# Tying DRAM-to-DRAM copies and accumulating DMAs of the up-projection's weights to their places in the ScalarE and GpSimd streams

## The chip, the core and the metric

The kernel runs on one core of a Trainium2 chip. The core has five engines that run their own instruction streams in order: TensorE (PE in the profile, its weight loads PEld), VectorE (DVE), ScalarE (ACT), GpSimd (POOL) and SyncE (SP). ACT, POOL and SP can issue DMAs, which run on the core's 16 DMA engines. The metric is the device time of one execution in microseconds; the number quoted is the median of several runs.

## The reference

A two-layer encoder on 1024 tokens of width 1024. Each layer adds three sub-layers to x: a mixer (latent attention, grouped-query attention and a gated MLP behind one input projection), cross-attention to 256 memory rows, and a gated feed-forward network (FFN) with a convolution over three tokens. The change touches the weights of the FFN's first product:

```python
def conv_gated_ffn(h, w_up, conv_w, conv_b, w_down):
    a = h @ w_up
    ap = jnp.pad(a, ((0, 0), (1, 1), (0, 0)))
    a = ap[:, :-2] * conv_w[0] + ap[:, 1:-1] * conv_w[1] + ap[:, 2:] * conv_w[2] + conv_b
    gate, val = a[..., :D_FF], a[..., D_FF:]
    return (jax.nn.silu(gate) * val) @ w_down

for l in range(DEPTH):
    x = x + hybrid_mixer(rms_norm(x, mix_norm[l]), ...)
    x = x + memory_cross_attention(rms_norm(x, mem_x_norm[l]), mem, ...)
    x = x + conv_gated_ffn(rms_norm(x, ffn_norm[l]), ffn_w_up[l], ...)
```

## The kernel before

All matrix products are done on pairs of rounded operands: a float32 tile is split into a high part (ACT or POOL copies it to the type fp32r) and a low part (DVE subtracts), and three matmuls add up one product (mm3, lines 113 to 115). `load` (lines 99 to 110) brings a weight tile in: SP issues the DMA (L103), POOL (L107) or ACT (L105) makes the high part, DVE (L108) the low part.

A layer runs in this order. First the opening: the input projection in four column groups, for the gated MLP (w_m; `gm_cols`, L414 to L424), keys and values (w_kv, L471), queries (w_q, L509) and the latent ranks (w_a, L543 to L548), with norms and rotary turns in between. Every norm needs a reciprocal root, which POOL computes as a power (L129, L560) from a DVE result and DVE then multiplies in (L420, L257, L563). Then the attention: 24 items of 512 queries and one head, 12 grouped-query and 12 latent ones; each item scores four tiles on PE (L733 and L734 for the first 12), takes the exponential on ACT (L296), scales by the sum on POOL (L302), transposes on PE (L137) and multiplies by the values (L315, L316). An item ends with L323 and L324 on ACT and L325 on POOL. Work for later items is filled in between from a table (`fill`). Then come the output projection, the memory attention and the FFN.

The FFN's up-projection is done with seven block products instead of eight (L1104 to L1106). The weights of products 1, 2 and 4 are blocks of w_up as they stand; those of 5, 6, 7 and 3 are sums of blocks: 5 is block 2 plus block 3, 6 is block 0 plus sum 5, 7 is block 0 plus block 2, and 3 is block 1 plus sum 6. These sums are made in DRAM, without any engine's arithmetic: `up_copy` (L778) has ACT issue a copy of one block's piece into a DRAM tile u, and `up_add` (L781) has POOL issue a DMA that adds another piece to it. Each sum is cut into six pieces, so a layer has 24 copies and 24 adds, of 512 KB or 1 MB. The FFN later reads u through SP (L1050).

In the code, the copies and adds are called inside the attention: `extra` gives step n (of 24) its copy in item n*5//6 and its add four items later, after the third tile of that item. The order of the instruction streams is not the order of the code, though: the framework's scheduler puts each engine's instructions in an order of its own, by priority and by when it reckons that their operands are there. A copy reads an input and writes a DRAM tile that nothing else uses before it, so for the scheduler it can go at any time. DMAs from ACT and SP share eight semaphore lanes; an issue that takes a lane waits for the DMA that had that lane before.

Of the kernel before, what the change touches and what calls it, by code (L numbers as in the profile page):

```python
# [11 lines left out]
ALU = mybir.AluOpType  # L12
# [57 lines left out]
def trunk(ctx: ExitStack, tc: tile.TileContext, a: dict, out: bass.AP):  # L70
    nc = tc.nc
# [319 lines left out]
    def layer(l, nt, last):  # L391
# [380 lines left out]
        up_sum = {(m, i): dpool.tile([P, n * CH + 16], F32, tag=f"u{l}_{m}_{i}", name=f"u{l}_{m}_{i}")[:, : n * CH] for m in (5, 6, 7, 3) for i, n in enumerate(UP_PARTS)}  # L772

        def up_piece(b, i):
            return a["w_up"][l, b][:, up_at[i] * CH : (up_at[i] + UP_PARTS[i]) * CH]

        def up_copy(m, i):
            nc.scalar.dma_start(up_sum[m, i], up_piece({5: 2, 6: 0, 7: 0, 3: 1}[m], i))  # L778

        def up_add(m, i):  # L780
            nc.gpsimd.dma_start(up_sum[m, i], {5: lambda: up_piece(3, i), 6: lambda: up_sum[5, i], 7: lambda: up_piece(2, i), 3: lambda: up_sum[6, i]}[m](), accum_op=ALU.add)  # L781

        def up_block(m, j):
            if m in (1, 2, 4):
# [58 lines left out]
        for n, (m, i) in enumerate(up_steps):  # L843
            extra.setdefault(n * 5 // 6, []).append(lambda m=m, i=i: up_copy(m, i))
            extra.setdefault(n * 5 // 6 + 4, []).append(lambda m=m, i=i: up_add(m, i))
# [537 lines left out]
```

## Time and profile before

| | us |
|---|---|
| median of 3 runs | 3009.76 |
| lowest, highest run | 3007.4, 3012.34 |
| the profiled execution, its span | 3010.89, 3008.9 |
| PE busy (share of the span) | 2807.4 (93%) |
| DVE, ACT, POOL busy | 1955.9, 1339.3, 650.0 |
| bytes moved by DMA | 297.61 MB, mean 99 GB/s |

The profile divides the span into 40 slices of 75 us and gives each engine's busy share, the clock that TensorE was granted (PEclk) and the use of the DMA engines. It lists instructions by line of the kernel; "s<-u" is a DMA from a DRAM tile u to a slot s. For each idle stretch of an engine it names the instruction or DMA that ended it. The times of layer 0 and of layer 1 can be set side by side, since both layers have the same code.

### The profile page before, as it was taken

The numbers are of one execution on the slowest core, as the hardware profiler recorded it, in microseconds if no ns is written. First come the engines' busy times: TensorE is split into PE (matmuls) and PEld (weight loads), VectorE is DVE, ScalarE is ACT, GpSimd is POOL, SyncE is SP. The second block draws the span as 40 slices with busy tenths as digits, with TensorE's granted clock in tenths as the row PEclk, the third lists the DMA queues.
The fourth block names the chain that finished last, engine by engine and source line by source line (L and its number), as shares of the span: only waits on it lengthen the run. The fifth ranks groups of instructions, "written<-read, shape, count | busy, mean of one in ns | idle before, by whom it ended". The sixth has DMA issues, their size and how long they took to land. (4 is left out here: it accounts for less than half of the span.)

```text
span 3008.9 us, 37081 instructions
## 1 busy us (share of the span) xinstructions
PE 2807.4 (93%) x13909; PEld 2358.4 (78%) x13909; DVE 1955.9 (65%) x2825; ACT 1339.3 (45%) x2572; POOL 650.0 (22%) x628
## 2 busy tenths in 40 slices
PE   3766499999999999999999999999999999999999
PEld 2656378888887888888888988888888788888887
DVE  2223489895667777777435489888466977778634
ACT  1212389882346444442104378985234644443101
POOL 2223245652200000002102245555111000001100
PEclk6878799999999999999999999999999999999999
DMA  9999920001211433334211000001111333335311
GB/s 311 256 251 265 245 72 1 1 29 57 71 57 56 143 121 123 126 130 171 98 42 39 23 14 1 1 8 50 53 54 59 110 126 125 120 121 191 123 56 56
DMA packets 93635, 297.61 MB, mean 99 GB/s; under 512 B 10384, under 2 KB 11024, under 8 KB 83216
## 3 DMA queue, kind: packets, MB, share of 16 engines
q1 hardware_dynamic: 79488, 202.70, 20.0%
q0 software_dynamic: 6912, 46.14, 7.8%
q10 hardware_dynamic: 7056, 46.40, 4.1%
q8 instruction: 110, 1.80, 0.2%
q14 instruction: 69, 0.57, 0.1%
HBM read 267.94 MB, written 119.54 MB: 129 GB/s over the span
## 5 line engine op out<-in xcount | busy, mean ns | idle before, releaser
L113 PE MATMUL bank<-s,s 128*128 128x512 f32 (+4 forms) x1831 | 684.8, 375 | 64.7 <-DVE s L121 36.3
L114 PE MATMUL bank<-s,s 128*128 128x512 f32 (+4 forms) x1831 | 678.8, 371 | 8.7 <-DVE s L108 8.7
L115 PE MATMUL bank<-s,s 128*128 128x512 f32 (+4 forms) x1831 | 679.7, 371 | 1.5 <-DVE s L108 1.4
L107 POOL TENSOR_SCALAR s<-s 128x1024 fp32r<-128x1024 f32 (+1 forms) x114 | 134.9, 1187 | 1456.0 <-DMA s<-in_w_down 1016.9
L113 PEld LDWEIGHTS bank<-s,s 128*128 128x128 f32 x1831 | 350.4, 192 | 121.8 <-DVE s L121 37.5
L114 PEld LDWEIGHTS bank<-s,s 128*128 128x128 f32 x1831 | 350.2, 191 | 60.2 <-DVE s L108 9.1
L137 PE MATMUL bank<-ident,s 128*128 128x128 f32 (+1 forms) x2320 | 321.9, 277 | 79.9 <-DVE stat L128 19.7
L121 DVE TENSOR_TENSOR s<-bank,s 128x512 fp32r<-128x512 f32 (+3 forms) x552 | 330.9, 630 | 99.7 <-ACT s L120 96.5
L115 PEld LDWEIGHTS bank<-s,s 128*128 128x128 f32 x1831 | 349.9, 191 | 54.6 <-DVE s L108 1.8
L120 ACT ACTIVATE s<-bank 128x512 fp32r<-128x512 f32 (+3 forms) x552 | 285.4, 555 | 207.1 <-PE bank L137 142.4
L137 PEld LDWEIGHTS bank<-ident,s 128*128 128x128 f32 (+1 forms) x2320 | 272.2, 141 | 134.2 <-issue 41.0
L108 DVE TENSOR_TENSOR s<-s,s 128x1024 fp32r<-128x1024 f32 (+4 forms) x172 | 214.3, 1255 | 125.4 <-POOL s L107 110.6
L1105 PE MATMUL bank<-s,s 128*128 128x512 f32 x704 | 274.5, 390 | 0.9 <-DVE s L206 0.9
L1106 PE MATMUL bank<-s,s 128*128 128x512 f32 x704 | 273.9, 389 | 0.0
L1104 PE MATMUL bank<-s,s 128*128 128x512 f32 x704 | 273.7, 389 | 0.0
L366 DVE TENSOR_TENSOR x<-x,bank 128x512 f32<-128x512 f32 x214 | 145.6, 684 | 193.4 <-PE bank L115 192.8
L302 POOL TENSOR_SCALAR s<-s,stat 128x1024 f32<-128x1024 f32 x192 | 218.5, 1141 | 224.3 <-DVE stat L301 156.3
L292 DVE TENSOR_REDUCE stat<-pair 128x1 f32<-128x1024 f32 x192 | 234.0, 1219 | 43.3 <-PE pair L734 23.3
L1057 ACT ACTIVATE s<-s 128x512 fp32r<-128x512 f32 x308 | 188.2, 628 | 162.7 <-PE bank L1106 49.7
L105 ACT ACTIVATE s<-s 128x1024 fp32r<-128x1024 f32 (+3 forms) x58 | 58.2, 1005 | 366.8 <-DMA s<-g 149.3
L296 ACT ACTIVATE s<-pair,stat 128x1024 f32<-128x1024 f32 x192 | 214.9, 1119 | 11.1 <-DVE stat L301 5.1
L1058 DVE TENSOR_TENSOR s<-s,s 128x512 fp32r<-128x512 f32 x308 | 201.8, 689 | 24.8 <-ACT s L1057 21.6
(164 smaller groups left out, 4659.8 us busy)
## 6 DMA issues: line engine op xcount, KB each, us to landing
s<-u SPq DMA_DIRECT2D x176, 256.0 KB, 3.0
u<-in_w_up ACTq DMA_DIRECT2D x40, 1024.0 KB, 19.2
s<-in_w_up SPq DMA_DIRECT2D x132, 256.0 KB, 3.2
g<-s SPq DMA_DIRECT2D x44, 512.0 KB, 2.8
s<-in_w_down SPq DMA_DIRECT2D x44, 512.0 KB, 4.8
s<-g SPq DMA_DIRECT2D x44, 512.0 KB, 5.6
u<-in_w_up POOLq DMA_DIRECT2D x20, 1024.0 KB, 18.4
u<-u POOLq DMA_DIRECT2D x20, 1024.0 KB, 19.8
```

The costliest lines, as they stand in the source:

```text
L113: nc.tensor.matmul(o, l[0], r[0], start=first, stop=False)
L114: nc.tensor.matmul(o, l[0], r[1], start=False, stop=False)
L115: nc.tensor.matmul(o, l[1], r[0], start=False, stop=last)
L120: nc.scalar.activation(hi, src, AF.Copy)
L121: nc.vector.tensor_tensor(lo, src, f(hi), ALU.subtract)
L137: nc.tensor.transpose(b[:m, j * P : (j + 1) * P], s, ident)
L292: nc.vector.reduce_max(self.nm[:, 0:1], s, axis=AX.X, negate=True)
L296: nc.scalar.activation(p, self.s, AF.Exp, bias=self.nm[:, 0:1], accum_out=self.den[:, t : t + 1])
L302: nc.gpsimd.tensor_scalar(p, p, r[:, 0:1], 0.0, ALU.mult, ALU.add)
L1104: nc.tensor.matmul(o, lh, rh, start=k == 0 and m in (1, 5, 6), stop=False, skip_group_check=True)
L1105: nc.tensor.matmul(o, lh, rl, start=False, stop=False, skip_group_check=True)
L1106: nc.tensor.matmul(o, ll, rh, start=False, stop=k == 3, skip_group_check=True)
```

## The change

Both DMA calls are handed to `tc.keep_in_program_order`, which holds an instruction at its place in its engine's stream: what the code issues on that engine ahead of it stays ahead, and what it issues behind it stays behind.

```diff
         def up_copy(m, i):
-            nc.scalar.dma_start(up_sum[m, i], up_piece({5: 2, 6: 0, 7: 0, 3: 1}[m], i))
+            tc.keep_in_program_order(nc.scalar.dma_start(up_sum[m, i], up_piece({5: 2, 6: 0, 7: 0, 3: 1}[m], i)))
 
         def up_add(m, i):
-            nc.gpsimd.dma_start(up_sum[m, i], {5: lambda: up_piece(3, i), 6: lambda: up_sum[5, i], 7: lambda: up_piece(2, i), 3: lambda: up_sum[6, i]}[m](), accum_op=ALU.add)
+            tc.keep_in_program_order(nc.gpsimd.dma_start(up_sum[m, i], {5: lambda: up_piece(3, i), 6: lambda: up_sum[5, i], 7: lambda: up_piece(2, i), 3: lambda: up_sum[6, i]}[m](), accum_op=ALU.add))
```

What this does to the streams shows at three places. The first is the start of the program on ACT, where L142 squares the first rows of x (a minus is a row of before that the changed stream doesn't have there; u_5_0 is piece 0 of sum 5):

```order
-L778 DMA u_5_0_1621<-in_w_up 128x1024
-L778 DMA u_5_1_1622<-in_w_up 128x2048
 L142 ACT_TABLE_LOAD
 L142 ACTIVATE s_2_115,stat<-x_78 128x1024
-L778 DMA u_7_0_1633<-in_w_up 128x1024
-L778 DMA u_6_0_1627<-in_w_up 128x1024
 L142 ACTIVATE s_3_123,stat<-x_79 128x1024
-L778 DMA u_6_1_1628<-in_w_up 128x2048
-L778 DMA u_7_1_1634<-in_w_up 128x2048
 L142 ACTIVATE s_4_131,stat<-x_80 128x1024
```

The copies left the start. In before all 48 copies, layer 1's too, stand among ACT's first 290 or so of some 2150 rows; now layer 0's stand from about row 180 to 570 and layer 1's from about row 1250 to 1640, between the instructions of their attention.

The second place is POOL in layer 0's opening, where the power for a key norm (L129, 16 columns) and two products of its rotary turn (L266, L268) stand; the tiles u with numbers above 13900 are layer 1's:

```order
-L781 DMA u_7_5_1638<-in_w_up 128x2048
-L781 DMA u_3_4_1643<-u_6_4_1631 128x2048
-L781 DMA u_3_5_1644<-u_6_5_1632 128x2048
-L781 DMA u_5_0_13916<-in_w_up 128x1024
 L129 TENSOR_TENSOR stat<-stat,mhalf 128x16
-L781 DMA u_5_1_13917<-in_w_up 128x2048
 L266 TENSOR_TENSOR s_89_1036<-s_74_705,s_73_703 128x512
 L268 TENSOR_TENSOR s_90_1037<-s_74_705,s_73_703 128x512
-L781 DMA u_7_0_13928<-in_w_up 128x1024
-L781 DMA u_6_0_13922<-u_5_0_13916 128x1024
```

The adds left the opening, and the power and the products follow one another without a DMA between them.

The third place is POOL in layer 1's attention, among the scalings of the exponentials (L302), an item's end (L325) and a sum of squares (L671):

```order
 L325 TENSOR_TENSOR s_1517_16274<-s_1518_16275 64x512
 L302 TENSOR_SCALAR s_1516_16268<-s_1516_16268,stat 128x1024
+L781 DMA u_6_3_13925<-u_5_3_13919 128x2048
+L781 DMA u_7_3_13931<-in_w_up 128x2048
+L302 TENSOR_SCALAR s_1521_16315<-s_1521_16315,stat 128x1024
 L671 TENSOR_TENSOR s_1483_15946<-s_1483_15946,s_1525_16367 128x1024
-L302 TENSOR_SCALAR s_1521_16315<-s_1521_16315,stat 128x1024
 L302 TENSOR_SCALAR s_1524_16361<-s_1524_16361,stat 128x1024
```

Adds now stand between scalings where there were none, and a few neighbours change places (here L302 goes ahead of L671). SP's stream stays as it was but for a few rows.

## Prediction, made before the changed kernel was run

> **What bounds the kernel now.** I read the slices of the page first.
>
> ```profile
> PE   3766499999999999999999999999999999999999
> PEclk6878799999999999999999999999999999999999
> DMA  9999920001211433334211000001111333335311
> GB/s 311 256 251 265 245 72 1 1 29 57 71 57 56 143 121 123 126 130 171 98 42 39 23 14 1 1 8 50 53 54 59 110 126 125 120 121 191 123 56 56
> ```
>
> From the sixth slice on PE is busy nine tenths and more: what could be won there is small. In the first five (375 us) PE is busy three to seven tenths, at a reduced clock, and the DMA engines are full. Which transfers fill them, two lines of the kernel tell (start times of their first and last DMA, and what POOL sat idle for ahead of its own):
>
> ```profile
> L778 ACTq DMA_DIRECT2D u<-in_w_up x48: 497/498/713, 0.7 to 384.4; - x48
> L781 POOL DMA_DIRECT2D u<-in_w_up x24: 807/842/1030, 6.4 to 372.8; - x24
> L781 POOL DMA_DIRECT2D u<-u x24: 809/848/1240, 35.0 to 390.4; - x24
>   DMA u<-in_w_up: 132.2, 25
> ```
>
> All 48 copies and 48 adds, both layers', run between 0.7 and 390 us, though the first FFN starts near 932 us. Third, layer 0 is set beside layer 1. Each row is a stretch: PE, PEld, DVE, ACT, POOL busy, clock, DMA share, GB/s. The pairs are the opening up to the end of attention's first item, the rest of the attention, and what lies between it and the FFN.
>
> ```profile
> 0.00:388.00 388.00, 219.73 (x1106) 195.97 (x1107) 119.70 (x191) 98.21 (x281) 106.54 (x120) 0.77 0.99 265
> 1605.00:1791.00 186.00, 182.33 (x1057) 167.81 (x1056) 108.08 (x165) 86.19 (x261) 62.49 (x58) 0.99 0.10 30
> 388.00:708.00 320.00, 313.68 (x1767) 260.33 (x1765) 278.08 (x472) 255.96 (x500) 171.87 (x158) 0.99 0.08 22
> 1791.00:2107.00 316.00, 311.82 (x1766) 258.86 (x1763) 277.38 (x473) 255.31 (x498) 171.70 (x157) 1.00 0.04 14
> 708.00:932.00 224.00, 220.93 (x1149) 187.89 (x1150) 127.03 (x187) 80.45 (x183) 33.00 (x37) 1.00 0.17 55
> 2107.00:2332.00 225.00, 221.96 (x1153) 188.53 (x1153) 127.82 (x190) 81.54 (x185) 32.30 (x37) 1.00 0.18 56
> ```
>
> The bounds of the stretches are the ends of first and last items (L323):
>
> ```profile
> L323 ACT ACTIVATE s<-bank x24: 592/595/601, 388.0 to 707.8; 64x512 f32<-64x512 f32 x24
> L323 ACT ACTIVATE s<-bank x24: 583/595/601, 1790.8 to 2107.0; 64x512 f32<-64x512 f32 x24
> ```
>
> Nearly the same PE work (1106 and 1057 matmuls) takes 388 us in layer 0 and 186 us in layer 1, where PE is 98% busy and the DMA engines a tenth. The other stretches agree. Layer 0's opening is the only place with much to win, and it has a twin that shows it undisturbed. Its waits, in total, number and longest, name two ways in which the transfers hold it:
>
> ```profile
> POOL s L107 <- DMA s<-in_w_q: 50.7, 4, 18.7
> ACT s L105 <- DMA s<-in_w_a: 45.5, 3, 17.9
> DVE s L257 <- POOL stat L129: 43.6, 4, 31.7
> DVE s L420 <- POOL stat L129: 41.2, 7, 14.7
> PE pair L733 <- DVE s L124: 23.1, 1, 23.1
> ```
>
> The weight loads land late behind the copies (the first two rows), and POOL, held by an add whose copy hasn't landed, can't compute the small power that DVE needs and PE after it (the other three).
>
> **What goes: the opening.** With the copies and adds gone from it, layer 0's opening should take layer 1's 186 us, plus what layer 1 doesn't have: the wait for the first data, 32 transposes of the first rows, and a cold clock.
>
> ```profile
> q1 hardware_dynamic: 2592, 7.50, 27.1%
> g<-s SPq DMA_DIRECT2D x44, 512.0 KB, 2.8
> 34.01 1.06 ACT L142 ACTIVATE s<-x 128x1024 f32<-128x1024 f32 x1 [15.51 <-DMA x<-in_x]
> 44.67 0.76 PE L113 MATMUL pair<-s,s 128*128 128x512 f32 x1 [0.23 <-ACT s L123]
> 45.66 0.63 PE L113 MATMUL pair<-s,s 128*128 128x512 f32 x1
> 56.51 0.39 PE L113 MATMUL pair<-s,s 128*128 128x512 f32 x1
> ```
>
> First data: SP's loads (q1, first 75 us) moved 7.50 MB in 27.1% of the engines' time, 369 GB/s. Four 512 KB rows of x then take 5.7 us; with the issue of the first (0.7 us) and a latency of 1.4 us (2.8 us for a lone 512 KB load, less its transfer) the fourth is there at 7.8 us instead of 34.0. From it to the first product took 10.7 us in before, with waits for POOL in it; that gives 18.5 us at most. The instructions alone in that chain come to some 5 us, so 12.8 at least. I take **14 us** for the start of the products (before: 44.67), nearer the lower end because the adds were what POOL waited for. The first weight tile comes 512 KB behind x and isn't later than this. Cold clock: equal matmuls last 0.63 us up to 56.1 us and 0.39 after, a slow stretch of 11.8 us, of which about half, **6 us**, is lost. The transposes: in layer 1's opening they cost 0.14 us each,
>
> ```profile
> L137 PE MATMUL bank<-ident,s 128*128 128x128 f32 x120 | 16.8, 274 | 1.0 <-DVE s L144 0.5 <-DVE s L121 0.3 <-DVE s L124 0.2
> ```
>
> so 32 of them **4.5 us**. Sum: 14 + 186 + 4.5 + 6 = 210.5 us, against 388: **177.5 us saved**. Bounds: 202 us (12.8 for the wait, no cold clock) to 236 (18.5, a cold stretch twice as long, and 15 us more because the first four tiles hang on DVE and ACT chains that layer 1 meets spread out). The last adds at 390 us also reach into the first items; 320 against 316 us says that this is worth another **4 us**.
>
> **What comes: 24 copies and 24 adds in each attention.** The transfers themselves: in the first 388 us the two queues show
>
> ```profile
> q10 hardware_dynamic: 6864, 45.88, 31.5%
> q0 software_dynamic: 6624, 44.04, 58.1%
> DMA to landing us min/median/max: 8.8/17.2/26.3
> ```
>
> 122 us of all engines for the 48 copies, and 225 us for 44 MB of adds, so about 179 us a layer in an attention of some 350 us, whose DMA engines are 4% busy. They fit. An add stands four items behind its copy; an item is 12.4 us (the two ends below), so a copy has 49 us, and adds that build on adds are two items or more apart, against at most 26.3 us from issue to landing even in the full queues. POOL shouldn't wait. The issues (POOL, ACT, and PE's worst wait for POOL in layer 1's attention):
>
> ```profile
> 416.47 1.29 POOL L325 TENSOR_TENSOR s<-s 64x512 f32<-64x512 f32 x1 [1.39 <-ACT s L324]
> 428.82 1.29 POOL L325 TENSOR_TENSOR s<-s 64x512 f32<-64x512 f32 x1 [1.35 <-ACT s L324]
> 386.56 0.83 POOL L781 DMA_DIRECT2D u<-u  x1 [5.04 <-DVE stat L301]
> 387.13 2.51 POOL L302 TENSOR_SCALAR s<-s,stat 128x1024 f32<-128x1024 f32 x2
> 357.51 0.50 ACTq L778 DMA_DIRECT2D u<-in_w_up  x1
> 357.68 0.81 ACT L601 ACTIVATE s<-bank 128x96 f32<-128x96 f32 x5
> PE bank L137 <- POOL s L302: 1.8, 2, 1.0
> ```
>
> An add holds POOL for 0.57 us (386.56 to 387.13) to 0.83, a copy ACT for 0 (L601 starts 0.17 us into the issue) to 0.5. Queued behind an add is the next scaling L302, and PE's transposes wait for that. At the dear end nothing is hidden: 24 x (0.83 + 0.5) = 32 us a layer. At the cheap end all is: POOL is idle 144 of 316 us, and PE waited 1.8 us for it in 24 items. ACT has less room (255 of 316 us busy), and the tying also moves some exponentials behind an item's end. I take 5 us a layer, nearer the cheap end by the row of PE's wait: **10 us lost**, between 0 and 64. If POOL's idle time were gone, the dear end would hold. Behind the attention nothing should change: the last add is issued in the last item, some 225 us ahead of the FFN that reads it.
>
> The sum is 177.5 + 4 - 10 = 171.5 us. The profiled execution took 3010.89 us (span 3008.9), 1.1 above the median of 3009.76; from the median, **2838 us**.
>
> **The rivals.**
>
> *The hold on POOL moves with the adds* (the one that ends slower). POOL's idle time ahead of its adds came to 132.2 us in 25 waits for copies alone, some 2.8 us for each of the 48; with the issue 3.6 us. If each add held POOL like that among the scalings and PE waited it out, 48 x 3.6 = 173 us would eat the 181.5 us won. From 3.8 us an add the kernel is slower; if every add waited as those 25 did, 5.3 us each, it would be 254 us, and 3082 us. Against it: 49 us of lead, and half-empty DMA engines. Half of the hold, some 85 us, would give 2923 us.
>
> *The opening is held by its own chains.* If tiles, not transfers, kept layer 0's loads back, only the first waits and half of the rest would go, some 90 us: 2920 us. Against it: layer 1's opening has the same tiles and waits for nothing.
>
> *VectorE locks GpSimd out of writing DMA descriptors.* DVE is busy 277 of 316 us in the attention; if each add had to wait out one long DVE instruction of 1.2 us,
>
> ```profile
> L292 DVE TENSOR_REDUCE stat<-pair 128x1 f32<-128x1024 f32 x192 | 234.0, 1219 | 43.3 <-PE pair L734 23.3
> ```
>
> and PE waited with it, 48 x 1.2 = 58 us would be lost on top: 2896 us. Against it: the add at 386.56 us, in the attention, took 0.83 us, under the median of 0.842. The Trainium skill's "SBUF — State Buffer", section "Who interferes with whom", states such a lock, for VectorE instructions in a two-port mode; by that rule this change would move the adds to where VectorE is busiest. The trace so far shows no add there that was slowed.
>
> *The change doesn't do what it says* is out: the streams show the DMAs moved.
>
> **How the numbers follow.** The forecast gets 0.80, from 3010 - 190 = 2820 to 3010 - 156 + 64 = 2918 us with all bounds at their ends. Half of the hold on POOL gets 0.08, held chains 0.06, the lock 0.03 (inside the range), the full hold and slower 0.03. The range is 2815 to 2900 us, which leaves out a little of the forecast's far end and most of the rivals. Faster by over 0.2% (what a measurement of this kernel can tell from no change) 0.96, the same 0.01, slower 0.03.
>
> **What would show it.** Right: the first slices of the DMA row fall to a tenth or two and the clock to nine tenths from the first or second slice; first L323 near 210 us; the first matmul near 14 us; DMA shares near a half in both attentions, whose lengths stay within 316 to 325 us; POOL's waits ahead of L781 near nothing. Wrong: PE waiting for L302 in the attention by tens of us (hold or lock; the lock shows as L781 above 1 us), or an opening above 236 us with DMA engines empty (chains).

## The result, and the profile after

The changed kernel takes 2870.75 us (median of 4 runs, 2869.55 to 2875.77) against 3008.61 us of the kernel before beside it: a ratio of 0.9543, 95% interval 0.9526 to 0.9559. The forecast was 2838 us, its range 2815 to 2900. The time lies inside the range and 33 us above the forecast. One cause, an order of instructions that the forecast didn't price, cost 39 us; the opening came out 5 us better than forecast and gave a part of that back.

First the slices of the changed kernel's page, the answer to the first view of before (a slice is now 72 us):

```profile
PE   9998999999999999999999989999999999999998
PEclk9999999999999999999999999999999999999999
DMA  4015676311133333531110157752221333335311
```

The clock stands at nine tenths or more from the first slice, and the wall of nines in the DMA row is gone. In its place stand two hills, one in each attention (slices 4 to 8 and 24 to 27). There PE has one slice of eight each. The lines of the copies and adds, and the windows (PE, PEld, DVE, ACT, POOL busy, clock, DMA share, GB/s), cut at the same events as in the prediction:

```profile
L778 ACTq DMA_DIRECT2D u<-in_w_up x48: 497/498/635, 177.2 to 1878.2; - x48
L781 POOL DMA_DIRECT2D u<-in_w_up x24: 789/832/1171, 236.4 to 1902.0; - x24
L781 POOL DMA_DIRECT2D u<-u x24: 762/808/1128, 264.3 to 1938.3; - x24
...
0.00:206.00 206.00, 196.24 (x1107) 177.96 (x1108) 125.07 (x191) 99.83 (x282) 69.08 (x73) 0.98 0.21 74
206.00:547.00 341.00, 318.52 (x1765) 260.20 (x1763) 286.17 (x473) 255.86 (x499) 191.97 (x180) 0.99 0.58 142
547.00:772.00 225.00, 222.12 (x1152) 188.44 (x1153) 126.95 (x189) 81.23 (x184) 34.64 (x37) 1.00 0.17 55
1446.00:1632.00 186.00, 181.58 (x1048) 167.38 (x1046) 106.37 (x164) 84.54 (x257) 61.10 (x57) 0.98 0.12 39
1632.00:1972.00 340.00, 318.60 (x1770) 260.94 (x1768) 285.29 (x473) 256.42 (x499) 194.26 (x181) 0.99 0.58 143
```

Layer 0's opening fell from 388 to 206 us. The two attentions rose from 320 and 316 to 341 and 340, although PE's busy time in them rose by 5 and 7 us only. The ends of the first and last items give the stretches exactly:

```profile
L323 ACT ACTIVATE s<-bank x24: 583/593/597, 205.6 to 546.7; 64x512 f32<-64x512 f32 x24
L323 ACT ACTIVATE s<-bank x24: 582/594/597, 1632.4 to 1972.1; 64x512 f32<-64x512 f32 x24
```

388.0 - 205.6 = 182.4 us won. The attentions took 341.1 and 339.7 us in place of 319.8 and 316.2: 21.3 + 23.5 = 44.8 us lost. That leaves 137.6 us. The two profiled executions differ by 135.3 us in their spans (3008.9 and 2873.6), a little less, because the stretch between the two attentions took 1085.7 us instead of 1083.0. The medians of all runs differ by 137.9. What PE waited for in the attentions (total, times, longest), layer 0 and layer 1 of the changed kernel, and last layer 1 of before:

```profile
PE bank L137 <- DVE s L121: 18.3, 17, 2.5
PE bank L137 <- DVE s L121: 18.1, 17, 2.6
PE bank L137 <- DVE s L121: 0.5, 2, 0.3
```

This is not a wait for POOL. The transposes (L137) want a PSUM bank (`bank`, which the matmuls write) that DVE frees when it has read the low part from it (L121). The row accounts for 17.6 of the 23.5 us that layer 1's attention lost; PE's own busy time, 6.8 us longer, covers the rest. A wait of PE for L302 is not among the rows of this view. One such gap, in the timeline of the changed kernel (start, length, engine, line, idle time ahead and its releaser):

```profile
1651.73 1.23 DVE L292 TENSOR_REDUCE stat<-pair 128x1 f32<-128x1024 f32 x1 [1.13 <-PE pair L734]
...
1652.22 0.60 ACT L120 ACTIVATE s<-bank 128x512 fp32r<-128x512 f32 x1 [0.45 <-PE bank L137]
1652.87 1.28 DVE L121 TENSOR_TENSOR s<-bank,s 128x512 fp32r<-128x512 f32 x2
1653.69 0.63 PE L137 MATMUL bank<-ident,s 128*128 128x128 f32 x4 [1.33 <-DVE s L121]
```

DVE stands idle for 1.13 us until a score tile is there for its reduce (L292), then reduces for 1.23 us, and only then takes the two low parts that free the banks. PE stands for 1.33 us. By the timeline, 10 of the 17 waits in layer 1's attention are of this kind, low parts right behind a reduce; they come to 12.7 of the 18.1 us. The order of DVE's stream at this place, in the changed kernel and then in the kernel of experiment x13, where only the copies' engine differs (stat_14617 is the reduce's result, s5_1352 and s2_1353 are the two low parts):

```
changed kernel
L301 RECIPROCAL stat_14586<-stat_14465 128x1
L292 TENSOR_REDUCE stat_14617<-pair_14612 128x1
L121 TENSOR_TENSOR s5_1352_14594<-bank_14589,s5_1352_14594 128x512
L121 TENSOR_TENSOR s2_1353_14602<-bank_14597,s2_1353_14602 128x512
L301 RECIPROCAL stat_14619<-stat_14465 128x1

copies issued by SP (x13)
L301 RECIPROCAL stat_14586<-stat_14465 128x1
L121 TENSOR_TENSOR s5_1352_14594<-bank_14589,s5_1352_14594 128x512
L121 TENSOR_TENSOR s2_1353_14602<-bank_14597,s2_1353_14602 128x512
L292 TENSOR_REDUCE stat_14617<-pair_14612 128x1
L301 RECIPROCAL stat_14619<-stat_14465 128x1
```

In the changed kernel the reduce went ahead of the two low parts. The diff doesn't touch either of them: the scheduler chose this order. Of layer 1's attention, 156 of 1981 PE rows and 63 of 489 DVE rows stand elsewhere than in before. (What was said of the tie where the change was introduced is too strong: it adds one edge, so that the DMA can't go ahead of the instruction that the code issued just before it on its engine. All others may still move.)

### The profile page after: what moved, and what is told of

The parts are those of the page before. It is cut to its first block, busy times and chain, and to the rows that moved or that the text cites. A ratio compares the mean times of both kernels' runs of the same rounds, so it can differ in the third digit from the quotient of the medians.

```text
span 2873.6 us, 37125 instructions
## 1 busy us (share of the span) xinstructions
PE 2798.3 (97%) x13909; PEld 2344.1 (82%) x13909; DVE 1975.6 (69%) x2825; ACT 1341.3 (47%) x2572; POOL 660.9 (23%) x628
## 5 line engine op out<-in xcount | busy, mean ns | idle before, releaser
L107 POOL TENSOR_SCALAR s<-s 128x1024 fp32r<-128x1024 f32 (+1 forms) x114 | 142.8, 1257 | 1374.3 <-DMA s<-in_w_down 1007.7
L121 DVE TENSOR_TENSOR s<-bank,s 128x512 fp32r<-128x512 f32 (+3 forms) x552 | 332.7, 631 | 109.1 <-ACT s L120 106.8
L113 PEld LDWEIGHTS bank<-s,s 128*128 128x128 f32 x1831 | 345.5, 189 | 62.7 <-DVE s L121 3.7
L115 PEld LDWEIGHTS bank<-s,s 128*128 128x128 f32 x1831 | 346.2, 189 | 53.8 <-DVE s L124 1.6
L114 PEld LDWEIGHTS bank<-s,s 128*128 128x128 f32 x1831 | 346.3, 189 | 50.9
L137 PE MATMUL bank<-ident,s 128*128 128x128 f32 (+1 forms) x2320 | 327.8, 276 | 45.5 <-DVE s L121 37.0
L137 PEld LDWEIGHTS bank<-ident,s 128*128 128x128 f32 (+1 forms) x2320 | 271.6, 141 | 108.0 <-issue 32.6
L302 POOL TENSOR_SCALAR s<-s,stat 128x1024 f32<-128x1024 f32 x192 | 224.5, 1169 | 249.1 <-DVE stat L301 159.6
L292 DVE TENSOR_REDUCE stat<-pair 128x1 f32<-128x1024 f32 x192 | 234.2, 1220 | 65.4 <-PE pair L734 38.0
L1104 PE MATMUL pair<-s,s 128*128 128x512 f32 x528 | 208.5, 395 | 1.2 <-ACT s L208 1.0
```

The lines of the kernel that those rows point to most:

```text
L113: nc.tensor.matmul(o, l[0], r[0], start=first, stop=False)
L114: nc.tensor.matmul(o, l[0], r[1], start=False, stop=False)
L115: nc.tensor.matmul(o, l[1], r[0], start=False, stop=last)
L121: nc.vector.tensor_tensor(lo, src, f(hi), ALU.subtract)
L137: nc.tensor.transpose(b[:m, j * P : (j + 1) * P], s, ident)
L292: nc.vector.reduce_max(self.nm[:, 0:1], s, axis=AX.X, negate=True)
```

## The experiments

x1, x3, x4, x6, x7, x9, x10 and x12 ran once each; the runs of one kernel, where there are several, lie up to 7.6 us apart (x11). The theory: the loss is the **order** of the neighbours. Its rivals: the DMAs themselves, by their **issue** on ACT and POOL or by their **traffic**. Where an order is imposed, every compute instruction of PE, DVE, ACT and POOL is chained to the one ahead of it as another build has it:

```diff
+def impose(tc):
+    ...
+        for d in steps:
+            at += d
+            if last is not None:
+                tc.add_manual_dep(mine[at], last.name, mybir.DependencyInfo(mybir.DependencyClass.NoSync, mybir.DependencyReason.DATA), reason="order")
+            last = mine[at]
         nt_ = layer(l, nt_, l == DEPTH - 1)
+    impose(tc)
```

These lines shift the numbers: L323 reads L349 there, L302 reads L328, L137 reads L163, L121 reads L147. In the kernels without sums the diff is this:

```diff
-            if m in (1, 2, 4):
-                return a["w_up"][l, {1: 0, 2: 1, 4: 3}[m]][:, j * CH : (j + 1) * CH]
+            if True:
+                return a["w_up"][l, {1: 0, 2: 1, 4: 3, 5: 2, 6: 0, 7: 2, 3: 1}[m]][:, j * CH : (j + 1) * CH]
...
-        for n, (m, i) in enumerate(up_steps):
-            extra.setdefault(n * 5 // 6, []).append(lambda m=m, i=i: up_copy(m, i))
-            extra.setdefault(n * 5 // 6 + 4, []).append(lambda m=m, i=i: up_add(m, i))
```

**x1: the changed kernel's order, no copies and adds.**

> Every engine's compute instructions stand in exactly the order of the changed kernel, imposed by a table, but the 48 copies and 48 adds are left out; the FFN reads plain blocks of w_up in place of the four sums (its output is another). Theory ORDER (the tied DMAs made the scheduler place the attention's instructions less well): both attentions stay at 340 us (first to last L323), PE waits some 18 us for L121 in each, about 2870 us in all. Theory ISSUE (holding ACT and POOL) and theory TRAFFIC (full DMA engines): both attentions fall to 316 us, about 2823 us.

**x2: the order of the build without copies and adds, all of them in.** The edit is `impose` alone.

> All copies and adds run in the attention as in the changed kernel, but the compute instructions of every engine stand in the order that the scheduler gives them when the DMAs are left out (imposed by a table). ORDER: attentions of 316 to 320 us, 2822 to 2832 us. ISSUE or TRAFFIC: attentions still about 340 us or worse, 2865 us or more.

**x3: no copies and adds, order left to the scheduler.**

> Copies and adds left out (the FFN reads plain blocks of w_up in place of the four sums), the scheduler free. All theories: attentions of 316 us as in layer 1 of before, about 2823 us; this is the floor for the attention with no sums to make.

The first and last items of x1, x2 and x3, both layers of each:

```profile
L349 ACT ACTIVATE s<-bank x24: 581/595/601, 205.7 to 541.6; 64x512 f32<-64x512 f32 x24
L349 ACT ACTIVATE s<-bank x24: 582/595/602, 1624.8 to 1959.8; 64x512 f32<-64x512 f32 x24
```
```profile
L349 ACT ACTIVATE s<-bank x24: 582/595/601, 204.4 to 525.8; 64x512 f32<-64x512 f32 x24
L349 ACT ACTIVATE s<-bank x24: 582/594/600, 1609.0 to 1934.9; 64x512 f32<-64x512 f32 x24
```
```profile
L323 ACT ACTIVATE s<-bank x24: 582/592/603, 206.1 to 522.0; 64x512 f32<-64x512 f32 x24
L323 ACT ACTIVATE s<-bank x24: 582/593/598, 1603.7 to 1919.6; 64x512 f32<-64x512 f32 x24
```

Without any DMA of these but with the changed kernel's order, the attentions take 335.9 and 335.0 us (2860.91 us in all); without both, 315.9 and 315.9 (2822.56). So **the order alone costs 20.0 and 19.1 us**. With the DMAs but without that order they take 321.4 and 325.9 us, 5.5 and 10.0 more than x3 and a little more than the 316 to 320 expected, and the kernel 2836.44 us (2832.33 to 2839.7, ratio 0.943, interval 0.9415 to 0.9446). The waits agree (layer 0, x1 and then x2):

```profile
PE bank L163 <- DVE s L147: 17.0, 15, 2.5
```
```profile
PE bank L163 <- POOL s L328: 4.0, 6, 1.6
PE bank L163 <- DVE s L147: 1.9, 3, 1.5
```

The long wait for the low parts comes with the order, DMAs or not. What the DMAs bring on their own is smaller: in x3 the two rows of x2 come to 1.8 and 0.2 us, so the wait for POOL's scaling, of which the forecast spoke, grew by 2.2 us and the one for the low parts by 1.7.

**x4: x2 with transfers of 8 KB.** In the DMA calls `up_sum[m, i]` becomes `up_sum[m, i][:, :16]`, the source likewise.

> The order of the build without DMAs on every engine, all 48 copies and 48 adds in their places, but each moves 16 columns (8 KB) instead of 1 MB; the FFN reads plain w_up blocks, so the sums are left out. It splits the 5.5 and 10 us an attention that the DMAs cost at the same order (321.4 and 325.9 us against 315.9). Theory 'issue': the instructions of ACT and POOL cost it, so both attentions take 320 to 326 us here too. Rival 'traffic': 1 MB transfers that fill half of the DMA engines cost it, so both take 316 to 317 us.

```profile
L349 ACT ACTIVATE s<-bank x24: 582/596/600, 205.0 to 526.1; 64x512 f32<-64x512 f32 x24
L349 ACT ACTIVATE s<-bank x24: 582/594/600, 1609.0 to 1931.5; 64x512 f32<-64x512 f32 x24
```

321.1 and 322.5 us: with 8 KB each, the issues cost 5.2 and 6.6 us an attention. In layer 0, PE's wait for the scaling is 1.5 us longer than in x3 (3.3 us), that for the low parts 1.7 (1.9 us), and PE's busy time 1.5 (313.6 us). The 1 MB transfers of x2 add 0.3 and 3.4. Layer 1's 3.4 us are not a wait but a slower PE, by x2's window:

```profile
1609.00:1935.00 326.00, 318.07 (x1767) 262.29 (x1766) 282.32 (x473) 255.62 (x499) 192.39 (x181) 0.98 0.60 149
```

In x4 PE is busy 314.62 us there, at a clock of 0.99. Whether the transfers brought the clock down isn't shown: x11 below, with as many bytes, has PE busy 314.40 us in that attention.

**x6: only the adds tied, the copies free.** The tie is taken off `up_copy`:

```diff
-            tc.keep_in_program_order(nc.scalar.dma_start(up_sum[m, i], up_piece({5: 2, 6: 0, 7: 0, 3: 1}[m], i)))
+            nc.scalar.dma_start(up_sum[m, i], up_piece({5: 2, 6: 0, 7: 0, 3: 1}[m], i))
```

> Of the change only the adds stay tied; the copies are free and go to the front of ScalarE's stream, into layer 0's opening. It splits the two ways in which the opening was held. Theory 'traffic': late loads alone held it; 48 copies cost 122 us of all DMA engines, a third of the 347 us of before, so the opening loses about a third of the 182 us that the change won: first L323 near 265 us. Rival 'held POOL': most of it was POOL standing behind adds, so first L323 comes by 225 us even with the copies in the opening. The attentions take about 340 us each by the order theory (adds tied alone move as many neighbours), 316 to 321 by a theory in which the two DMAs of a pair cost it.

**x7: the kernel before with transfers of 8 KB.** Nothing is tied; the DMA calls are cut as in x4.

> The kernel before, nothing tied, so that all 48 copies and 48 adds stay in layer 0's opening, but each moves 16 columns (8 KB); the FFN reads plain blocks, so the sums are left out. The number of issues in the opening stays, the traffic goes. Theory 'traffic': first L323 at 206 to 225 us. Rival 'issue and hold': 48 adds of 0.84 us and what POOL stands for them stay, so first L323 stays above 245 us (206 + 48 x 0.84).

First and last items of layer 0, x6 and then x7:

```profile
L323 ACT ACTIVATE s<-bank x24: 580/596/600, 230.4 to 557.3; 64x512 f32<-64x512 f32 x24
```
```profile
L323 ACT ACTIVATE s<-bank x24: 582/593/599, 233.1 to 549.4; 64x512 f32<-64x512 f32 x24
```

x7 splits the 182 us of the opening: with every issue in place but no traffic it takes 233.1 us, so traffic (with the holds that it causes) was 155 us of it and the issues alone 27. 233.1 us lie between the two theories' figures. x6 shows that traffic isn't paid by the byte: the 48 copies, a third of what stood there, cost 25 us and not 60. Its DMA engines were 71% busy in the first 231 us, before's 99%, and POOL waited 18.5 us for w_q there, against 50.7 in before. By its forecasts x6 speaks for the held POOL (225 us) rather than for late loads alone (265). How the 155 us divide between loads that landed late and a POOL that stood behind adds, no run separates. The expectation of x6 for the attentions fell too: 326.9 and 323.5 us, not 340. The adds' tie alone moves 118 PE rows in layer 1's attention (the change 156) and costs little. So the price isn't in the number of rows that move.

**x9: only the copies tied, the adds free.** The tie is taken off `up_add`.

> Of the change only the copies stay tied; the adds are free to go as early as the copy they add to. With the adds alone tied the attentions took 326.9 and 323.5 us, with both 341.1 and 339.7. Theory 'a place held on ScalarE turns the neighbours' order': the copies' ties make most of the loss, so the attentions take 333 us or more here, and PE waits 10 us or more an attention for L121. Rival 'the adds' ties, or only both together': 316 to 327 us.

2916.91 us, with attentions of 359.3 and 364.3. PE's waits in layer 1's attention:

```profile
PE bank L137 <- DVE s L121: 20.9, 14, 4.6
PE bank L137 <- POOL s L302: 7.3, 4, 3.8
```

By x6 and x9 the copies' tie is the harmful one. x9 isn't clean, though: its adds stand right behind their copies, POOL waited 71.2 us for copies ahead of the adds, which may account for the second row, and the clock in its attentions was 0.97 and 0.96, against 0.99 in the changed kernel.

**x10 and x13: the change with its copies issued by SP.** One word of the change:

```diff
-            tc.keep_in_program_order(nc.scalar.dma_start(up_sum[m, i], up_piece({5: 2, 6: 0, 7: 0, 3: 1}[m], i)))
+            tc.keep_in_program_order(nc.sync.dma_start(up_sum[m, i], up_piece({5: 2, 6: 0, 7: 0, 3: 1}[m], i)))
```

> The change with its copies issued by SyncE (SP) instead of ScalarE, tied to the same places in the program; the adds stay tied on GpSimd; order left to the scheduler. ScalarE's stream then holds no tied instruction. Theory 'a place held on ScalarE turns the neighbours' order': attentions as with the adds alone tied, 323 to 328 us, no opening in front of 210 us, and 2840 to 2848 us in all. Rival 'both DMAs of a pair, wherever they are issued': 335 us or more and 2865 to 2875 us.

> The kernel with the copies on SyncE once more, for an interval: its one time was 2839.25 us. If that time holds, 2836 to 2842 us, a ratio to the kernel before of 0.943 to 0.945, with attentions of 323.8 us each; that is the change without its loss of order, 29 to 34 us below the changed kernel.

x10 took 2839.25 us; x13, the same kernel, 2838.31 (2833.75 to 2839.76, 5 runs, ratio 0.9432, interval 0.942 to 0.9445). Of x13 the items and the wait in layer 1, and where the gap of the changed kernel was:

```profile
L323 ACT ACTIVATE s<-bank x24: 582/592/597, 203.0 to 524.3; 64x512 f32<-64x512 f32 x24
L323 ACT ACTIVATE s<-bank x24: 583/594/599, 1607.5 to 1930.4; 64x512 f32<-64x512 f32 x24
```
```profile
PE bank L137 <- DVE s L121: 2.1, 5, 0.9
```
```profile
1623.96 1.27 DVE L121 TENSOR_TENSOR s<-bank,s 128x512 fp32r<-128x512 f32 x2
...
1625.14 1.22 DVE L292 TENSOR_REDUCE stat<-pair 128x1 f32<-128x1024 f32 x1
...
1625.33 0.60 PE L137 MATMUL bank<-ident,s 128*128 128x128 f32 x4
```

The low parts go first again, the transposes don't wait, and the attentions take 321.3 and 322.9 us. SP runs ahead of the other engines, so layer 0's copies all go out between 160.8 and 214.2 us, at the end of the opening; there they cost nothing that shows.

**x12: the change as it is, with transfers of 8 KB**, to tell the tie from the bytes that the scheduler sees.

> The change as it is, copies on ScalarE and adds on GpSimd tied to their places, order left to the scheduler, but each DMA moves 16 columns (8 KB); the FFN reads plain blocks, so the sums are left out. In the built program only 19 of some 1980 TensorE rows of layer 1's attention move against the order without DMAs, where the changed kernel moves 156. If the scheduler turns the order because it reckons with the bytes of the tied copies, the attentions take 320 to 324 us here, as with the free order and 8 KB, and 2830 to 2838 us in all. If the tie itself makes the loss, whatever the size, they take 335 us or more.

```profile
L323 ACT ACTIVATE s<-bank x24: 583/593/598, 205.0 to 525.0; 64x512 f32<-64x512 f32 x24
L323 ACT ACTIVATE s<-bank x24: 582/592/597, 1608.5 to 1930.6; 64x512 f32<-64x512 f32 x24
```

320.0 and 322.1 us, 2835.83 in all, and PE's wait for L121 in layer 1 is 1.2 us. The tie alone doesn't make the loss: with the same ties at the same places the order stays nearly that of x3 and the loss of 20 us is gone. Since x2 carries the full traffic without that loss, it isn't the traffic on the chip. It is the size as the scheduler sees it, for copies tied on ACT. (x12 also feeds the FFN plain blocks. That isn't it: the changed kernel with this one edit, its DMAs at full size, builds to the same order of compute instructions as the changed kernel.) How the scheduler reckons with the size wasn't looked into.

**x8 and x11: two ways to get the last 5 to 10 us.** x8 imposes the order of x3 and moves layer 1's sums into layer 0's FFN:

```diff
+            if l == 0 and i % 5 == 0 and i // 5 < 24:
+                up_copy(1, *up_steps[i // 5])
+            if l == 0 and i % 5 == 0 and 4 <= i // 5 < 28:
+                up_add(1, *up_steps[i // 5 - 4])
```

> The order of the build without DMAs imposed on every engine, layer 0's copies and adds in its attention as in the change, layer 1's copies and adds moved into layer 0's FFN (a copy every fifth product, its add four copies later). If the DMAs at a given order cost only where they stand among an attention's items, layer 1's attention goes back to 316 us and the kernel takes 2826 to 2830 us, 8 to 10 less than with both in the attentions (2836). If the FFN's products, whose blocks are loaded over the same DMA engines, pay for the traffic, it takes 2836 us or more.

x11 is x2 with the copies on SP.

> Both remedies: the order of the build without DMAs imposed on every engine, and the copies issued by SyncE. With that order and copies on ScalarE the attentions took 321.4 and 325.9 us, with transfers of 8 KB 321.1 and 322.5, without DMAs 315.9 both. If ScalarE's issues (24 of 0.5 us at most) are what the attentions still pay, they take 317 to 319 us and the kernel 2826 to 2830 us; if GpSimd's issues are (24 of 0.81 to 0.85 us), they stay at 321 to 326 us and the kernel within 3 us of 2836.

x8 took 2845.92 us (2844.12 to 2850.27). Layer 1's attention fell to 318.3 us, but from layer 0's last item to layer 1's first it took 1099.1 us instead of x2's 1083.2. The windows of x8 and then x2 over the FFN:

```profile
750.00:1440.00 690.00, 677.56 (x2981) 555.43 (x2981) 459.90 (x579) 243.25 (x339) 60.61 (x59) 0.99 0.59 177
```
```profile
750.00:1440.00 690.00, 687.32 (x3053) 564.72 (x3052) 473.81 (x597) 250.32 (x354) 45.06 (x45) 1.00 0.33 111
```

PE did 10 us less in the same 690 us. Two waits of that stretch stand out in x8 (L428 is the add, L1088 makes the high part of a block of w_up):

```profile
POOL u L428 <- DMA u<-in_w_up: 324.7, 23, 27.8
ACT s L1088 <- DMA s<-in_w_up: 23.4, 6, 9.5
```

x2 has no wait like the second row, so in x8 blocks did land late. The first row, POOL standing at adds whose copies hadn't landed, may have cost nothing: in x2 POOL stood 504.4 us of the same stretch waiting for loads of w_down (x8: 176.6). So the traffic is the likely cause of the 16 us, but no run separates it from that hold. x11 took 2836.14 us (2831.01 to 2838.58), attentions 321.5 and 324.5: ACT's issues are not what is still paid, since without them nothing fell clearly. x2, x11 and x13 can't be told apart, and all three beat both kernels.

| kernel | opening | attention of layer 0 | of layer 1 | us |
|---|---|---|---|---|
| changed kernel | 205.6 | 341.1 | 339.7 | 2870.75 |
| x1, its order without DMAs | 205.7 | 335.9 | 335.0 | 2860.91 |
| x2, order of x3 with DMAs | 204.4 | 321.4 | 325.9 | 2836.44 |
| x3, no DMAs | 206.1 | 315.9 | 315.9 | 2822.56 |
| x12, ties with 8 KB | 205.0 | 320.0 | 322.1 | 2835.83 |
| x13, copies on SP | 203.0 | 321.3 | 322.9 | 2838.31 |

## Why the prediction was right, and where it was off

*The opening* was right, and for its reason. 210.5 us were forecast from layer 1's 186 and four terms, and 205.6 came. The first of these can be checked by itself: the products were to start at 14 us. From the changed kernel's timeline:

```profile
14.22 0.85 PE L113 MATMUL pair<-s,s 128*128 128x512 f32 x2 [0.54 <-ACT s L123]
17.28 0.97 PE L115 MATMUL pair<-s,s 128*128 128x512 f32 x2
18.09 0.39 PE L113 MATMUL pair<-s,s 128*128 128x512 f32 x1
```

Products of 0.39 us come from 18.09 us on, so the slow stretch was 3.9 us long and not 11.8. By the prediction's half that is 2 us instead of 6, most of the 5 us by which the opening came in lower. Of the two ways in which the transfers held the opening, late loads and a held POOL, the runs don't tell the shares. The rival of held chains (2920 us) is out.

*The 4 us for layer 0's attention* were right: without copies and adds it takes 315.9 us like layer 1 (x3), against 319.8 in before.

*The cost of the issues* was right in size: 5 us a layer were forecast, and x4 measured 5.2 and 6.6. The place that the prediction named, PE's wait for the scaling, is 1.5 us of that. The transfers fit, as it said: they add 0.3 and 3.4 us, the latter at a lower clock.

*The term that was mis-sized* is the sum of what comes in the attentions. "I take 5 us a layer" meant the issues, with the words "the tying also moves some exponentials behind an item's end" beside it, and **no price for that**. The order that the scheduler made around the tied copies cost 20 us a layer (x1 against x3). Attentions of 316 to 325 us were forecast; 341 and 340 came. Over x3, 25.2 + 23.8 = 49.0 us stand in place of 10: the order's 20.0 and 19.1, and 5.2 and 4.7 for the DMAs at that order (after against x1). The bounds of 0 to 64 us held this, but only because the dear end had been worked out for another cause, every issue unhidden. That the time still fell into the range is in this part luck. The test that the prediction set itself pointed the wrong way as well: it looked for PE waiting on L302, and the wait was on L121, in rows of DVE that no view of before could have shown. The order of the two streams, which did show them, was read for where the DMAs went; the few neighbours that it saw change places got no price.

*The hold on POOL* didn't move with the adds. POOL has no wait for a copy among its rows in the attentions; the lead of four items was enough. x9 shows what happens without that lead. *The lock* of GpSimd by VectorE didn't show: the adds now stand where DVE is busy 286 of 341 us, and their medians are 0.832 and 0.808 us, against 0.842 and 0.848 in the opening of before. By the prediction's own sign, adds above 1 us, there are 9 of 48, at most 1.17 us, against 4 in before, at most 1.24: too few and too short for the 58 us of that rival. What lengthened these 9 isn't known. The Trainium skill's "SBUF — State Buffer", section "Who interferes with whom", states such a lock for VectorE instructions in a two-port mode. No run here shows one.

## What to carry to other kernels

A change that holds an instruction at its place also moves its neighbours where a scheduler sets the order; compare the streams for rows that the diff doesn't name, and give those on the path a price of their own: here reduces that went ahead of reads which free a bank cost some 13 of the 20 us an attention, and the DMAs' issues 5. Before blaming a transfer, run the new order without it and the old order with it; two runs tell them apart. If an engine at work on the path need not issue a DMA, try an idle queue for it. Here that paid because the scheduler's order stayed good (x13), not because the issues themselves had cost ACT time (x11).

## What the runs showed of the hardware

The same kind of traffic cost very different times. The 48 copies in the opening cost 25 us at a DMA share of 0.71 (x6); copies and adds together, at 0.99, cost 182, of which the issues were 27 (x7). How much of that is the full engines and how much the adds that held POOL, these runs don't separate. And a stretch with room on the DMA engines on average isn't a cheap one: one layer's sums cost an attention 5 to 10 us, but in the FFN, whose own loads come to a DMA share of 0.33, they cost some 16 (x8), although the two together came to no more than 0.59. There too POOL stood at adds, waiting for their copies.
